# First two units behind each change of operands interleaved product by product, with weights and sums prepared in DRAM

## The chip, the cores and the metric

One core of one Trainium2 chip. The metric is the device time of the whole program in microseconds. The kernel before was run three times: 1918.71, 1915.92 and 1916.36 us, a median of 1916.36. One more execution was taken with the hardware profiler.

## The reference

A hybrid decoder layer on x (2048 tokens x 1024 channels, float32). One projection of the normalised input gives the parts of a gated short convolution, of a windowed attention, and of the merge gates; each branch is multiplied by a gate and projected back, and the merged result is projected once more.

```python
h = rms_norm(x, norm_g)
v_c, b_c, c_c, z_c, q, k, v, z_a, gate_logits = split(h @ w_in)
y_c = b_c * causal_depthwise_conv(c_c * v_c, conv_w) * silu(z_c)
y_a = y_c @ w_conv_out
o   = sliding_window_attention(rms(q), rms(k), v, sinks) * silu(z_a)   # window 128, 16 heads, 4 kv heads
y_b = o @ w_attn_out
g_a, g_b = split(sigmoid(gate_logits + gate_b))
return x + (g_a * y_a + g_b * y_b) @ w_out
```

## The kernel before

**Tiles and units.** The 2048 tokens are two tiles of T = 1024 (t = 0, 1). The work is a chain of units. A unit is 256 output channels for the 1024 tokens of a tile (in the last projection, o, 256 tokens for 1024 channels). Every float32 operand is split into a high part, rounded to fp32r by a cast on ScalarE (L279), and a low part, the rest, by a subtraction on VectorE; a product of two operands is hi.hi + hi.lo + lo.hi.

**Seven products or eight.** `sunit` (L493) is one level of Strassen's scheme in Winograd's form: seven products of half-size blocks, in the order 1, 5, 6, 2, 7, 3, 4. One product (`product`, L476, matmul L482) is 4 x 3 = 12 matmuls of 128x512. X, V and Y are banks of partial sums: product 1 goes to X and is copied by ScalarE to Y (L500); product 5 goes to V and is copied to s5 (L509); product 6 adds to Y, and VectorE sets V = s5 + Y; products 2, 7, 3 and 4 then complete the four blocks of the output, (0,0) in X, (1,1) as Y + s5, (0,1) in V and (1,0) in Y. The moving operands of the products are op 1, 2, 3 (plain blocks of the input) and op 5, 6, 7, 4 (their sums and differences), each of four pieces j = 0 to 3; "operand 2_3" is piece 3 of op 2. A plain unit is the ordinary block product: four outputs of two products, eight products and 96 matmuls, with op 1, 2, 3 and 8 (the fourth plain block).

**Changes of operands.** All units that share an input use one set of operands. At a change of input the set has to be formed anew: 28 or 32 splits and 16 sums. Per tile, and in this order (but for ga_0 of t = 0, which comes ahead of q), these are the units: k, v, q (on the normalised x), cv and b (with attention woven in), ga, gb, z, za (on the normalised x), then yb (the attention's output, operands ophc), then ya (the convolution's, operands ophy in t = 1; in t = 0 ya is the plain `branch`, L1255); after both tiles o (operands ophwo, from w_out; the merged rows are its weights). The first unit behind a change is plain, since that needs only plain blocks at first: yb_0 in both tiles (`yb_first`, L1279, matmul L1296), ya_0 in t = 1 and o_0 (`qunit`, L528, matmul L542). In t = 0 ga_0 is plain too.

**Order of the work.** The program is written out tick by tick: `run` (L676) gives one product of a unit per tick and calls what `put(n, f)` placed at that tick: operand splits, sums, loads. Tables of ticks (CSUM_AT, CONV_AT, WO_FORM_AT and others) place them. Beside that each tick prepares one piece of a coming unit's weights (`pieces_of`): from a raw tile of 1 MB, loaded by SP a unit or two ahead (L347), ScalarE casts 128x1024 high parts and VectorE subtracts the low parts (`ah`, `al` for products 1 and 2, `sh`, `sl` for 6 and 5, `th`, `tl` for 7 and 3, `d` for 4) and forms the sums. They live in eight tiles that are used in turn. Each engine then works its own list in order; a DMA issued by SP waits in SP's list for its data, and what stands behind it waits too.

**Ends of units.** yb's and ya's outputs are multiplied by a gate (th, loaded from gd in DRAM) and go to mt in DRAM: yb's by a store on SP (L1329), ya's by an accumulating DMA on POOL (L1331). The gate's tiles come from a pool of two. The last projection adds xr (a piece of x) and stores out (L1381). In t = 0's and t = 1's z and za units the attention of the tile's last blocks is still running (scores L1023, exponentials L1052, transposed through DRAM as fd, L1072 and L1079).

**The opening.** The statistics of x's norm are worked out in the first 40 us; TensorE transposes rtok (L609) so that rb can scale the tokens of a column block.

## Time and profile before

| what | value |
|---|---|
| runs | 1918.71, 1915.92, 1916.36 us (median 1916.36) |
| the profiled execution's own time | 1914.36 us |
| its span from the first to the last instruction | 1912.6 us |
| TensorE (PE) | 8718 matmuls |
| DMA | 371.79 MB, mean 194 GB/s |

Times in the views are microseconds from the span's start. In a row of the chain or the timeline the first number is the start, the second the duration; "x12" counts instructions, and what stands in brackets is the engine's idle time before the row and what ended it. In a row of the windows each engine's busy time is followed by its count of instructions, then the granted clock, the busy share of the DMA engines, and GB/s. L482 is line 482 of the kernel.

### The profile page before, as it was taken

How to read it: one execution, taken by the hardware profiler on the slowest of the kernel's cores; microseconds unless marked ns; L12 is line 12 of the kernel's file. 1: busy time of each engine (PE TensorE's matmuls, PEld its weight loads, DVE VectorE, ACT ScalarE, POOL GpSimd, SP SyncE). 2: the span in 40 equal slices, each digit the busy share in tenths (PEclk: the TensorE clock that was granted, in tenths of full speed). 3: DMA queues.
4: the chain of work that ended last, by engine and by line, in shares of the span. 5: the costliest groups of instructions: out<-in, count | busy, mean ns of one | idle time of the engine just before them, and what ended most of it. 6: DMA issues, size and time to landing. Idle time of an engine off the chain costs nothing.

```text
span 1912.6 us, 27255 instructions
## 1 busy us (share of the span) xinstructions
PE 1900.8 (99%) x8718; PEld 1581.7 (83%) x8718; DVE 1540.4 (81%) x2614; ACT 991.0 (52%) x1969; POOL 589.4 (31%) x850
## 2 busy tenths in 40 slices
PE   9999999999999999999999999999999999999999
PEld 7888888888887888888888888888888888888887
DVE  7988888898878669669799888888998578777854
ACT  7665555456657444434565544556666335434321
POOL 2083425345565000011462333445555001121000
PEclk9999999999999999999999999999999999999999
DMA  8286455558787433894585554567776674688453
GB/s 301 72 244 182 153 164 171 169 175 248 231 251 225 163 111 135 282 280 117 171 229 151 176 158 141 162 219 241 234 243 213 219 243 159 229 268 205 151 175 112
DMA packets 209279, 371.79 MB, mean 194 GB/s; under 512 B 28592, under 2 KB 103344, under 8 KB 199152
## 3 DMA queue, kind: packets, MB, share of 16 engines
q1 hardware_dynamic: 174688, 281.63, 44.9%
q0 software_dynamic: 30848, 79.99, 15.7%
q10 hardware_dynamic: 3600, 8.42, 1.3%
q8 instruction: 70, 1.15, 0.3%
q14 instruction: 73, 0.60, 0.1%
HBM read 252.22 MB, written 117.72 MB: 193 GB/s over the span
## 4 chain that ended last, share of the span: by engine, by line
PE 90%; DVE 4%; DMA 4%; issue 1%; ACT 0%; SPq 0%; POOL 0%; DVEq 0%; ACTq 0%; POOLq 0%
PE Y L482 33%; PE Vcv L482 4%; PE Xcv L482 4%; PE ya L1255 4%; PE Xgb L482 2%; PE Vq L482 2%; PE Xq L482 2%; PE yb L1296 2%; PE po L1117 2%; PE Vgb L482 2%; PE Vz L482 2%; PE Xz L482 2%; PE Vo L482 2%; PE Xo L482 2%; PE Vb L482 2%; PE Xb L482 2%
## 5 line engine op out<-in xcount | busy, mean ns | idle before, releaser
L1079 POOL DMA_DIRECT2D x<-fd x256 | 139.6, 552 | 120.5 <-DMA fd<-f 63.2
L1052 ACT ACTIVATE p<-s,st,rq 128x128 f32<-128x128 f32 x256 | 113.0, 450 | 5.4 <-DMA fd<-f 5.3
L1072 POOL DMA_DIRECT2D fd<-f x64 | 36.9, 576 | 229.1 <-DVE f L248 214.7
L1100 POOL TENSOR_SCALAR_AFFINE_SELECT xh<-xh 64x512 fp32r<-64x512 f32 x64 | 58.8, 919 | 147.4 <-DVE xl L248 104.4
L1351 POOL DMA_DIRECT2D mt<-tha x16 | 13.8, 860 | 257.6 <-DVE tha L248 244.3
L482 PE MATMUL Xcv<-oph,wcv_ah 128*128 128x512 f32 x256 | 79.2, 390 | 0.0
L1100 POOL TENSOR_SCALAR_AFFINE_SELECT xl<-xl 64x512 fp32r<-64x512 f32 x64 | 65.1, 1018 | 4.4
L1100 POOL TENSOR_SCALAR_AFFINE_SELECT yp<-yp 64x512 fp32r<-64x512 f32 x64 | 58.1, 908 | 4.2
L248 DVE TENSOR_TENSOR o<-po,o 64x256 f32<-64x256 f32 x128 | 53.3, 417 | 4.3 <-ACT o L1129 3.4
L1100 POOL TENSOR_SCALAR_AFFINE_SELECT yp<-xl 64x512 fp32r<-64x512 f32 x64 | 55.8, 872 | 3.1
L482 PEld LDWEIGHTS Xcv<-oph,wcv_ah 128*128 128x128 f32 x256 | 47.6, 188 | 9.6
L375 ACT CAST wcv_sh<-wcv_raw 128x1024 fp32r<-128x1024 f32 x16 | 16.8, 1052 | 70.5 <-DVE wcv_raw L248 70.5
L1817 POOL DMA_DIRECT2D oc<-ocd x16 | 8.7, 541 | 142.2 <-DMA th<-gd 118.9
L248 DVE SCALAR_TENSOR_TENSOR y<-u,cols,y 128x512 f32<-128x512 f32 x64 | 49.7, 776 | 3.4 <-ACT y L1166 2.2
L1129 ACT COPY o<-po 64x256 f32<-64x256 f32 x128 | 47.1, 368 | 8.3 <-PE po L1117 3.9
L248 DVE TENSOR_TENSOR p<-p,st 128x512 f32<-128x512 f32 x64 | 48.4, 756 | 3.1
L1052 ACT ACTIVATION_READ_ACCUMULATOR p<-s,st,rq 128x1 f32 x256 | 50.6, 198 | 0.0
L857 POOL DMA_DIRECT2D q2d<-q_h x64 | 44.2, 690 | 20.1 <-ACT q_h L852 11.0
L482 PE MATMUL Xcv<-oph,wcv_al 128*128 128x512 f32 x128 | 49.8, 389 | 0.0
L248 DVE TENSOR_TENSOR ophc<-zain,ophc 128x512 fp32r<-128x512 f32 x64 | 42.2, 687 | 7.1 <-ACT ophc L279 7.1
L248 DVE STREAM_TRANSPOSE f<-p 128x512 f32<-128x512 f32 x64 | 45.5, 711 | 3.0 <-DMA q<-q2d 0.2
L1027 PEld LDWEIGHTS s<-kq,q 128*128 128x128 f32 x256 | 45.9, 189 | 2.2
(698 smaller groups left out, 6539.3 us busy)
## 6 DMA issues: line engine op xcount, KB each, us to landing
gd<-th SPq DMA_DIRECT2D x64, 256.0 KB, 3.0
wcv_raw<-in_w_units SPq DMA_DIRECT2D x16, 1024.0 KB, 5.3
q<-q2d SPq DMA_DIRECT2D x64, 256.0 KB, 4.8
v<-vd SPq DMA_DIRECT2D x128, 128.0 KB, 3.4
fd<-f POOLq DMA_DIRECT2D x64, 256.0 KB, 4.3
x<-fd POOLq DMA_DIRECT2D x256, 64.0 KB, 3.3
th<-gd SPq DMA_DIRECT2D x48, 256.0 KB, 5.5
wga_raw<-in_w_units SPq DMA_DIRECT2D x8, 1024.0 KB, 7.0
```

What stands on the lines that cost most here:

```text
L248: r = f(*args, **kw)
L482: nc.tensor.matmul(ps, lhsT=w[:, j, :], rhs=b[:, m, :], start=start and j == 0 and i == 0, stop=j == KP - 1 and i == 2, skip_group_check=n ...
L857: nc.gpsimd.dma_start(q2d[t][j][half, q * 2 * HB : (q + 1) * 2 * HB, i, e, :], src[HALVES[e]].bitcast(F32).rearrange("p (b x) -> p b x", x ...
L1027: nc.tensor.matmul(sp[:, h, c, skip : 3 * HD], lhsT=q2[:, h, c, :], rhs=kq[:, 0, keys], start=False, stop=c == 1)
L1052: nc.scalar.activation(out=p[:, i, :], in_=sg[:, i, HD : 3 * HD], func=AF.Exp, bias=st[:, 1, i : i + 1], scale=rv[:, i // 2, i % 2 : i % 2 ...
L1072: nc.gpsimd.dma_start(fd, f)
L1079: nc.gpsimd.dma_start(x[QUADS[k]], src[k])
L1100: nc.gpsimd.affine_select(out=d4, in_=s4, pattern=[[0, 2], [-32 * sg, 2], [0, G], [-sg, 32]], compare_op=ALU.is_gt if prev else ALU.is_ge, ...
L1117: nc.tensor.matmul(po[:, cs], lhsT=v2[:, kind, :], rhs=xx[:, :, h * HD : (h + 1) * HD], start=n == 0, stop=n == 2)
L1129: nc.scalar.copy(ov, pov[oth, :, e])
L1255: nc.tensor.matmul(ps, lhsT=w[:, j, cs], rhs=o[:, m, :], start=n == 0 and i == 0, stop=n == KC - 1 and i == 2)
L1296: nc.tensor.matmul(banks[i, q], lhsT=w[:, j, :], rhs=b[:, l, :], start=n == 0 and m == 0, stop=n == KC - 1 and m == 2, skip_group_check=True)
```

## The change

**Pairs.** At each of the four changes (yb in t = 0 and 1, ya in t = 1, o) the first two units are run together by `spair`: product 1 of the first, product 1 of the second, then 2, 2, 5, 5, 6, 6, 3, 3, 7, 7, 4, 4. Both have seven products; op 8 isn't formed any more. The first unit uses the banks as before; the second has X and V in banks of the pool ps_m and its own bank for Y. ga_0 of t = 0 stays plain.

**Prepared weights.** In t = 0's z and za units `prepare` forms all high and low parts of yb_0's and yb_1's weights once (22 VectorE operations, 14 casts) and stores them in DRAM (wpd, 28 stores of 256 KB). The yb pairs of both tiles load them from there (kind "L", 14 loads of 512 KB a pair) in place of 1 MB raw a unit with casts and subtractions.

**Sums of w_out.** `wo_sums` forms them in t = 1's z and za units and stores them in DRAM (wsd); at the o change 28 pieces of 256 KB are loaded, each three ticks ahead of its split.

**Places.** The pieces of the weights of a pair alternate between its units. The second transposes of rtok move from tick 11 to 12, and the other places of the opening stay where they were, now in a table. Attention blocks 29 to 31 of t = 0 load a tick earlier. CSUM_AT, CONV_AT, WO_FORM_AT and the ticks of yb's operands (CA_...) have new numbers. `sunit` has a flag `last` for an order 1, 5, 6, 7, 2, 4, 3; it is given as `n + 1 == len(zs)`, after loops in the same body that set n to other values.

DMAs on SP: 1166 before, 1260 after; on POOL 580 and 576. VectorE has 2620 instructions after, 2614 before.

```diff
-TURNED_AT = (6, 11)
+TURNED_AT = (6, 12)
+WO_AHEAD = 3
+EARLY_LOADS = ((0, 29), (0, 30), (0, 31))
+PAIR = (1, 2, 5, 6, 3, 7, 4)
...
+    def prepare(key, n0, places):
...
+        def high(m, kh, over):
+            r = raw[kh]
+            hi = slot([P, H], F32R, f"wph_{w}_{j}_{m}")
+            lo = (r if over else slot([P, H], F32, f"wpl_{w}_{j}_{m}")).bitcast(F32R)
+            nc.scalar.copy(hi, r)
+
+            def low():
+                vec.tensor_tensor(out=lo, in0=r, in1=hi.bitcast(F32), op=ALU.subtract)
+                put(tick[0] + 1, keep)
+
+            def keep():
+                for l, v in enumerate((hi, lo)):
...
+                    nc.sync.dma_start(to, v.bitcast(F32))
+
+            put(tick[0] + 1, low)
...
+        if kind == "L":
+            made = wpd[key[0], key[2]]
+
+            def fetch(ms, i):
+                def go():
...
+                        tiles = wpair(f"{name}_{'ast'[i]}")
...
+                    for l, v in enumerate(tiles):
+                        nc.sync.dma_start(v.bitcast(F32), made[i][:, l])
+
+                put(tick[0] + 1, go)
+                return (lambda: None, lambda: None)
...
+    def spair(keys, ops, fins, order):
...
+        xb, vb, yb, s5 = [None, None], [None, None], [Y, None], [None, None]
+        for n, e in ((n, e) for n in order for e in range(2)):
+            u, fin, nm = us[e], fins[e], nms[e]
+            if n == 1:
+                xb[e] = (mb if e else bank)(f"X{nm}")
+                product(xb[e], u, 1, ops, True)
+                if e:
+                    yb[e] = bank(f"Y{nm}")
+                nc.scalar.copy(yb[e], xb[e])
+            elif n == 2:
+                product(xb[e], u, 2, ops, False)
+                fin(0, 0, xb[e])
+            elif n == 5:
+                vb[e] = mb(f"V{nm}")
+                product(vb[e], u, 5, ops, True)
+                s5[e] = spare(f"s5{nm}")
+                nc.scalar.copy(s5[e], vb[e])
+            elif n == 6:
+                product(yb[e], u, 6, ops, False)
+                add(vb[e], s5[e], yb[e])
...
+            yield
...
-    def yb_first(t, ops, fin):
...
+    def wo_sums(n, j):
...
+        def out(m, a, b, c):
+            sub(a, b, c)
+            nc.sync.dma_start(wsd[m, j], a)
...
+        for i, (m, j) in enumerate((m, j) for m in PAIR for j in range(KP)):
+            n = n1 + WO_FORM_AT[i]
+            put(n - WO_AHEAD, lambda m=m, j=j: ld(m, j))
+            put(n, lambda m=m, j=j: op_split("wo", m, j, got[m, j], st["ops"]))
...
-            put(n - 5, step("l", lambda g, j=j, b=b: att_load(t, j, b)))
+            put(n - 5 - ((t, r) in EARLY_LOADS), step("l", lambda g, j=j, b=b: att_load(t, j, b)))
...
-            run(sunit((key, t, j), ops, fin))
+            run(sunit((key, t, j), ops, fin, last=n + 1 == len(zs)))
...
-        run((sunit if n else qunit)(("o", n), state[NT]["ops"], fin))
+    run(spair([("o", e) for e in range(2)], state[NT]["ops"], [fins[e][0] for e in range(2)], PAIR))
...
+        run(sunit(("o", n), state[NT]["ops"], fin))
```

TensorE at the start of yb in t = 1, before the change: the end of the first and all of the second of the plain unit's last four outputs, yb_1_0, by op 1 and 2 (ophc) with the plain weights p1h and p1l, and the next unit's first product.

```order
L1296 MATMUL yb_1_0_15772<-ophc_1_0_15522,wyb_0_p1h 128x512 x2
L1296 MATMUL yb_1_0_15772<-ophc_1_0_15522,wyb_0_p1l 128x512
...
L1296 MATMUL yb_1_0_15772<-ophc_1_3_15615,wyb_0_p1h 128x512 x2
L1296 MATMUL yb_1_0_15772<-ophc_1_3_15615,wyb_0_p1l 128x512
L1296 MATMUL yb_1_0_15772<-ophc_2_3_15684,wyb_0_p1h 128x512 x2
L1296 MATMUL yb_1_0_15772<-ophc_2_3_15684,wyb_0_p1l 128x512
L482 MATMUL Xyb_1_15813<-ophc_1_0_15522,wyb_1_ah 128x512 x2
L482 MATMUL Xyb_1_15813<-ophc_1_0_15522,wyb_1_al 128x512
```

The same place after: products 1 and 1 are over with the first four rows, and product 2 of the first unit follows, up to operand 2_3.

```order
L632 MATMUL Xyb_1_15795<-ophc_1_2_15678,wyb_1_ah 128x512 x2
L632 MATMUL Xyb_1_15795<-ophc_1_2_15678,wyb_1_al 128x512
L632 MATMUL Xyb_1_15795<-ophc_1_3_15735,wyb_1_ah 128x512 x2
L632 MATMUL Xyb_1_15795<-ophc_1_3_15735,wyb_1_al 128x512
L632 MATMUL Xyb_0_15764<-ophc_2_0_15727,wyb_0_ah 128x512 x2
L632 MATMUL Xyb_0_15764<-ophc_2_0_15727,wyb_0_al 128x512
L632 MATMUL Xyb_0_15764<-ophc_2_1_15778,wyb_0_ah 128x512 x2
L632 MATMUL Xyb_0_15764<-ophc_2_1_15778,wyb_0_al 128x512
L632 MATMUL Xyb_0_15764<-ophc_2_2_15781,wyb_0_ah 128x512 x2
L632 MATMUL Xyb_0_15764<-ophc_2_2_15781,wyb_0_al 128x512
L632 MATMUL Xyb_0_15764<-ophc_2_3_15810,wyb_0_ah 128x512 x2
L632 MATMUL Xyb_0_15764<-ophc_2_3_15810,wyb_0_al 128x512
```

Operand 2_3 was read first at the end of the plain unit's sixth product and is now read at the end of the pair's third.

ScalarE around the cast of that operand, before (zas_7_0 is the gate that completes the last block of the attention's output):

```order
L1223 ACTIVATE zas_7_0_15630<-Y 128x512
L279 CAST ophc_2_2_15632<-zain_2_1_0_15286 128x512
L375 CAST wyb_1_ah<-wyb_1_raw 128x1024
L279 CAST ophc_8_3_15657<-zain_3_0_1_15418 128x512
L279 CAST ophc_3_3_15660<-zain_3_1_1_15416 128x512
L375 CAST wyb_1_d<-wyb_1_raw 128x512
L279 CAST ophc_2_3_15684<-zain_3_1_0_15420 128x512
```

And after:

```order
L1427 ACTIVATE zas_7_0_15750<-Y 128x512
L303 CAST ophc_5_2_15752<-zain_2_0_0_15397 128x512
L704 COPY Y<-Xyb_0_15764 128x512
L303 CAST ophc_2_1_15778<-zain_1_1_0_15256 128x512
L303 CAST ophc_2_2_15781<-zain_2_1_0_15403 128x512
L303 CAST ophc_3_3_15789<-zain_3_1_1_15545 128x512
L704 COPY Yyb_1_15808<-Xyb_1_15795 128x512
L303 CAST ophc_2_3_15810<-zain_3_1_0_15549 128x512
```

The casts of weights are gone from the place, and the two copies of X into Y now stand between the casts of operands.

SP in the yb pair of t = 1, after (wpd holds the prepared weights, gd the gates, mt takes the products of yb's outputs and gates):

```order
L484 DMA wyb_1_sh<-wpd_yb_1_5959 128x1024
L484 DMA wyb_1_sl<-wpd_yb_1_5959 128x1024
L1495 DMA th_0_1_15792<-gd_1_119 128x512 x2
L1508 DMA mt_115<-th_0_0_15761 128x512 x2
L484 DMA wyb_0_th<-wpd_yb_2_5956 128x1024
L484 DMA wyb_0_tl<-wpd_yb_2_5956 128x1024
L1495 DMA th_0_2_15881<-gd_1_119 128x512 x2
L484 DMA wyb_1_th<-wpd_yb_2_5960 128x1024
L484 DMA wyb_1_tl<-wpd_yb_2_5960 128x1024
L484 DMA wyb_0_d<-wpd_yb_3_5957 128x1024
L1508 DMA mt_115<-th_0_1_15792 128x512
```

The same place before:

```order
L347 DMA wyb_2_raw<-in_w_units 128x2048
L1317 DMA th_0_0_15637<-gd_1_118 128x512 x2
L1317 DMA th_0_1_15664<-gd_1_118 128x512 x2
L1329 DMA mt_114<-th_0_0_15637 128x512 x2
L1329 DMA mt_114<-th_0_1_15664 128x512
L1317 DMA th_1_0_15785<-gd_1_118 128x512 x2
L1329 DMA mt_114<-th_0_1_15664 128x512
L347 DMA wyb_3_raw<-in_w_units 128x2048
```

One raw load of 1 MB per unit, two units ahead, gave way to loads for the pair itself, some of which stand behind stores of the same pair.

More of the change, by code (lines that the diff above doesn't have):

```diff
@@ L513, in sunit @@
         yield
-        if not two:
+        if not two and not last:
             product(xb, u, 2, ops, False)
@@ L520, in sunit @@
         yield
[L521 to L523 removed]
+        if last:
+            product(xb, u, 2, ops, False)
+            fin(0, 0, xb)
+            yield
+        else:
+            product(vb, u, 3, ops, False)
+            fin(0, 1, vb)
+            yield
         product(Y, u, 4, ops, False)
@@ L1333, in y_unit @@
-        if j:
-            return sunit(key, ops, fin), get
-        return (yb_first(t, ops, fin) if w else qunit(key, ops, fin)), get
+            last = shared and n == len(order) - 1
+            pair = None if last else upool.tile([P, 2 * H + 2], F32, tag="u", name=f"th{w}{t}_{js[0]}_{n}")
+            for e, (j, i, q) in enumerate(order[n]):
+                th[j, i, q] = slot([P, H], F32, f"th{w}{t}_{j}_{n}") if last else pair[:, hs(e)]
+                nc.sync.dma_start(th[j, i, q], gd[t][w][2 * j + i, :, hs(q)])
@@ new lines, in y_ends, with y_units @@
+        return [fin_of(j) for j in js], get
+    def y_units(t, w, ops):
+        key = "yb" if w else "ya"
+        order = PAIR
+        outs = pair_outs(order)
+        fins, get = y_ends(t, w, (0, 1), outs)
+        units = [(spair([(key, t, j) for j in range(2)], ops, fins, order),
+                  get, ((0, 0), (1, 1), (outs[0][0] + 1, 2), (THS_AT, 3)), outs[1][0] + 1)]
+        for j in range(2, NJ):
+            (fin,), get = y_ends(t, w, (j,), None)
+            units.append((sunit((key, t, j), ops, fin), get, ((0, 0), (1, 1)), 7))
+        return units
@@ L1767, in block_kernel @@
         zs[0][3]()
+        if t + 1 == NT:
+            for j in range(KP):
+                wo_sums(tick[0] + WO_SUMS_AT[j], j)
+        if t == 0:
+            for j in range(2):
+                prepare(("yb", j), tick[0], (PREP_A, PREP_B)[j])
         def csum(n, j):
```

479 lines of the change are left out of this document (294 added, 185 removed).

## The prediction

> **What bounds the kernel now.** I read the page's busy shares first, then the chain that ended last, then TensorE's waits, then windows around the four places that the change touches.
>
> ```profile
> span 1912.6 us, 27255 instructions
> ...
> PE 1900.8 (99%) x8718; PEld 1581.7 (83%) x8718; DVE 1540.4 (81%) x2614; ACT 991.0 (52%) x1969; POOL 589.4 (31%) x850
> ...
> PE 90%; DVE 4%; DMA 4%; issue 1%; ACT 0%; SPq 0%; POOL 0%; DVEq 0%; ACTq 0%; POOLq 0%
> ```
>
> PE is busy for 1900.8 of 1912.6 us, so 11.8 us is all its idle time, and the chain runs through it. A matmul that goes is time that goes, as long as the operands keep up. The chain at the changes of operands (the one of t=1 in full) shows whether they do:
>
> ```profile
> 725.07 21.76 PE yb L1296 x96
> ...
> 1596.12 21.76 PE yb L1296 x96
> 1617.88 2.72 PE Xyb L482 x12
> 1620.60 2.72 PE Vyb L482 x12
> ...
> 1675.00 21.76 PE Qya L542 x96
> ...
> 1753.88 21.76 PE Qo L542 x96
> ```
>
> Each plain unit takes 21.76 us for 96 matmuls, 0.2267 us each, and a product of 12 takes 2.72 us. Rows follow without a gap: 1596.12 + 21.76 = 1617.88. The windows say the same, and show how near VectorE is to its limit there:
>
> ```profile
> core 0: us, PE busy (x) PEld busy (x) DVE busy (x) ACT busy (x) POOL busy (x), PEclk, DMA share, GB/s
> ...
> 725.00:763.00 38.00, 38.00 (x170) 31.45 (x169) 36.30 (x57) 17.65 (x30) 0.00 (x0) 1.00 0.38 132
> ...
> 1596.00:1634.00 38.00, 38.00 (x169) 31.49 (x168) 36.31 (x57) 17.71 (x30) 9.73 (x18) 1.00 0.64 224
> ...
> 1675.00:1713.00 38.00, 38.00 (x169) 31.45 (x169) 27.44 (x41) 12.76 (x21) 10.97 (x17) 1.00 0.85 260
> 1713.00:1754.00 41.00, 41.00 (x183) 33.94 (x182) 29.20 (x42) 20.42 (x31) 8.54 (x10) 1.00 0.96 246
> 1754.00:1792.00 38.00, 38.00 (x169) 31.48 (x168) 36.41 (x57) 13.09 (x21) 0.85 (x1) 1.00 0.49 143
> ```
>
> PE has no idle time and a full clock in any of them; VectorE is busy for 36.3 of 38 us. So the question is what feeds the shorter stretch.
>
> **Term 1, the matmuls.** Four plain units of eight products become units of seven: 4 x 12 = 48 matmuls, 8718 to 8670, at 0.2267 us: **-10.88 us**. Two units now take 14 products, 14 x 2.72 = 38.08 us, where they took 40.80.
>
> **Term 2, the opening.**
>
> ```profile
> 38.99 0.62 PE L609 MATMUL ptr<-ident,rtok 128*128 128x128 f32 x4 [1.52 <-DVE rtok L603]
> ...
> 67.85 0.69 DVE L248 TENSOR_TENSOR oph<-xt,oph 128x512 fp32r<-128x512 f32 x1
> ...
> 68.73 0.61 PE L542 MATMUL Qga<-oph,wga_p0h 128*128 128x512 f32 x2
> ```
>
> The second transposes of rtok stand 12 matmuls later (2.7 us), past the 1.52 us that PE waited for rtok. But VectorE's low part of operand 3_3 ends at 68.54, and the matmul that reads it is the second of the pair at 68.73, about 68.96. VectorE's chain is not shortened, so with PE 1.5 us earlier this operand is about 1 us late. Between 0 and -1.5; I take **-0.5 us**.
>
> **Term 3, the pairs' own operands.** Their times come from walking each engine's new order from the pair's start, with these durations:
>
> ```profile
> 1674.40 1.66 ACT L279 CAST ophy<-oc 128x512 fp32r<-128x512 f32 x3
> ...
> 1675.64 1.89 DVE L248 TENSOR_TENSOR ophy<-oc,ophy 128x512 fp32r<-128x512 f32 x3
> ...
> 1677.44 1.22 DVE L248 TENSOR_TENSOR wya_al<-wya_raw,wya_ah 128x1024 fp32r<-128x1024 f32 x1
> ...
> 1678.58 0.69 DVE L248 TENSOR_TENSOR ophy<-oc,ophy 128x512 fp32r<-128x512 f32 x1
> ...
> 1699.51 0.57 ACT L500 COPY Y<-Xya 128x512 f32<-128x512 f32 x1 [4.29 <-PE Xya L482]
> ```
>
> Back to back, a VectorE operation of 128x512 takes (1.89 - 0.69) / 2 = 0.60 us, one of 128x1024 1.14 (1677.44 to 1678.58), a cast 0.52; a copy starts 0.03 us behind its product's end (1699.48) and takes 0.57.
>
> In the yb pair VectorE has 51 operations, three of them 128x1024: 48 x 0.60 + 3 x 1.14 = 32.2 of 38.08 us. It had 36.3 in 38. Weight work left (prepared in t=0), so on the mean it keeps up. The tight point is the place shown for ScalarE: the copy of X into the new bank Yyb stands ahead of operand 2_3's cast. Product 1 of the second unit ends at 5.44; copy to 6.04, cast to 6.6, low part to 7.4; its reader, the 11th matmul of product 2, stands at 5.44 + 10 x 0.2267 = 7.71. That leaves 0.3 us, where the plain unit read 2_3 only in its sixth product. Operand 4_1 comes out at 33.6 against 33.5. Both yb pairs: 0 to 1 us; I take **+0.4**.
>
> Their loads: VectorE's and ScalarE's work on two units' weights becomes 14 loads of 512 KB. The later ones wait on SP behind stores of mt that wait for VectorE; in before such stores held SP 31 times, for 112.3 us in all and 15.9 at most:
>
> ```profile
> SPq L1329 <- DVE th L248: 112.3, 31, 15.9
> ```
> ```profile
> wya_raw<-in_w_conv_out SPq DMA_DIRECT2D x8, 512.0 KB, 7.1
> ...
> wya_raw<-in_w_units SPq DMA_DIRECT2D x4, 1024.0 KB, 7.2
> ...
> wo<-in_w_out SPq DMA_DIRECT2D x16, 256.0 KB, 6.9
> ```
> ```profile
> xr<-in_x SPq DMA_DIRECT2D x32, 256.0 KB, 4.0
> ...
> oc<-csd POOLq DMA_DIRECT2D x16, 256.0 KB, 5.1
> ```
>
> By the walk wyb_0_th goes out at about 11.7 (behind the store that needs product 2 of the second unit, 10.88) and is needed at 21.76; wyb_1_th at 14.6, needed at 24.48; wyb_1_d at 25.5, needed at 35.36. Each has about 10 us, and 512 KB landed in 7.1: no cost, with 3 us to spare.
>
> The ya pair (t=1) still forms its weights. Its narrow point is the last low part of operand 7_3, at 28.9 against 29.5, behind the cast of the third unit's weights, whose load goes out at 15.2. At 7.2 us it fits, at 10 us VectorE's queue would end 2.5 late: 0 to 2.5, I take **+0.5** (nearer the 7.2).
>
> The o pair: operand 7_3's load goes out at about 16.4, behind a store that waits for product 2 of the second unit and VectorE's queue. With 5.1 us it lands at 21.5; cast, low part, 4_2's low part, a 128x1024 one and the sum for V follow (0.6 + 0.7 + 0.6 + 1.1 + 0.7) to 25.2, where product 3 of the second unit wants V at 24.48: 0.7 late. With 4.0 us nothing is late, with 6.9 it is 2.5. Operand 4_0, loaded behind the next weights, adds 0 to 1.5. So 0 to 4; DMA is at 0.49 in that window of before, so I take 5.1 and 0.5: **+1.2**.
>
> [...]
>
> **Term 4, what is made ahead.** The weights of yb_0 and yb_1 get 22 VectorE operations (13 us) and 14 casts in t=0's z and za units, with 2 MB loaded and 7.3 MB stored; w_out's 16 sums (10 us) and 8 MB move to t=1's.
>
> ```profile
> 620.00:660.00 40.00, 40.00 (x181) 33.23 (x180) 23.22 (x33) 15.49 (x25) 3.31 (x4) 1.00 0.59 210
> 660.00:700.00 40.00, 40.00 (x179) 33.10 (x178) 22.01 (x29) 14.56 (x22) 0.00 (x0) 1.00 0.29 106
> ...
> 1460.00:1500.00 40.00, 40.00 (x186) 33.43 (x185) 29.27 (x40) 19.60 (x33) 10.05 (x13) 1.00 0.54 179
> 1500.00:1540.00 40.00, 40.00 (x178) 32.86 (x177) 25.40 (x36) 14.13 (x22) 0.00 (x0) 1.00 0.72 249
> ```
>
> From 620 to 700 VectorE is free for 34.8 us and the DMA engines for more than half; from 1460 to 1540 it is free for 25. The cover is there. SP gets 34 and 24 more DMAs at 0.33 us each:
>
> ```profile
> 1699.29 0.33 SPq L347 DMA_DIRECT2D wya_raw<-in_w_units  x1
> ```
>
> That is 19 us over some 250; behind them stand only loads for the next unit, 19 us ahead of it (seven products). Were the cover gone, the last attention blocks would pay, as one did before:
>
> ```profile
> 575.28 0.46 ACT L1052 ACTIVATE p<-s,st,rq 128x128 f32<-128x128 f32 x1 [5.30 <-DMA fd<-f]
> ...
> 577.21 0.44 PE L1023 MATMUL s<-lows,kq 128*128 128x384 f32 x1 [2.18 <-ACT p L1052]
> ```
>
> This 2.18 us can go (three blocks of t=0 load a tick earlier) or come twice: -2.2 to +2.2, I take **0**.
>
> **Sum.** -10.88 - 0.5 + 0.4 + 0.5 + 1.2 + 0 = **-9.3 us**. The profiled execution took 1914.36 (span 1912.6 and 1.8 outside it): 1905.1. The runs shown have a median of 1916.36, 2.0 above it; on that basis **1907.1 us**. The terms at their best give -10.88 - 1.5 - 2.2 = -14.6 (1901.8), at their worst -10.88 + 1 + 2.5 + 4 + 2.2 = -1.2 (1915.2).
>
> **Rivals.** *The operands of the pairs are late, and most of the gain is stall.* A set of four operands is now due every 5.44 us, and each pair has a place with under 0.7 us to spare; if VectorE runs 1.5 us behind my walk at each pair (its queue is in order, so a delay stays), the four pairs lose 6 and the o pair its 2 to 4 more: -10.88 + 9 = about -2, **1914.5**. For it: VectorE's 36.3 of 38 us before. Against it: the 6 us less that it now has. Chance 0.11.
>
> *The prepared weights' loads land too late, and it is slower.* Place: the 512 KB loads issued from 11.7 on in the two yb pairs.
>
> ```profile
> 1626.00:1636.00 10.00, 10.00 (x46) 8.28 (x45) 9.83 (x15) 3.16 (x6) 4.25 (x9) 1.00 1.00 364
> ```
>
> The DMA engines were already full once in that stretch, at 364 GB/s. Each load has 10 us; product 3 and then, issued later for it, product 4 wait for what is over that, so a pair loses 2 x (L - 10) for a landing of L. It is slower than before from L = 10 + 9.3 / 4 = 12.3 us, and by over 0.2% from 13.3; at 16 us it is 24 - 9.3: **1931**. Against it: 7.1 us for 512 KB, and 4 MB of oc loads that stood in that window now start later. Chance 0.07.
>
> *The change does less than it says*: the opening gives back its 1.5 us and the order with a last product moved in za's last unit does not take effect (its flag compares a loop variable that inner loops have set anew, and the new order shows the old products). Both are in the sum already; **1907.6**, inside the forecast.
>
> *The clock falls in the pairs.* They rotate over six banks of partial sums. In this trace the clock was 1.00 in every window, and a wait of 2.18 us did not lower it. If a stall halved it for one product behind it, each would cost 1.36 us, in four pairs with two stalls 11: **1918**, within 0.2%. [...] Chance 0.02.
>
> **How the numbers follow.** Forecast 0.80, rivals 0.11, 0.07 and 0.02. A measurement here tells about 0.2% (3.8 us) from no change: faster means below 1912.5, slower above 1920.2. The forecast is faster but for its worst corner (0.03), the late operands divide (0.03 faster, 0.08 same), the clock is same, the loads slower, and 0.01 of the same is moved to slower for what I have not seen: faster 0.80, same 0.12, slower 0.08. The range takes in the terms' ends, 1902 to 1915.
>
> **What would show it.** PE x8670 and about 1890 us busy; chain rows of 2.72 through all four pairs, 38.08 us each; TensorE's idle time near 13 us, with its waits in the pairs on ophc's low part, on Vo and on ophwo 7_3 or 4_0. Waits of PE on wyb loads would make the slower rival; waits over 2 us on VectorE in each pair the first; a wait near 69 us on oph shows the opening giving back.

## The result and the profile after

| | before | after |
|---|---|---|
| median of the runs | 1916.36 us (9 runs, 1913.82 to 1918.71) | 1911.87 us (9 runs, 1909.72 to 1915.00) |
| ratio | | 0.9979, 95% interval 0.9970 to 0.9988 |
| profiled execution, its span | 1914.36, 1912.6 us | 1912.3, 1910.6 us |

The change gains 4.5 us, 0.2%. The sign and the main term are as forecast, the size is half: -9.3 was expected. First the page of the kernel after, its busy times and the engines' shares of the chain:

```profile
span 1910.6 us, 27374 instructions
...
PE 1894.5 (99%) x8670; PEld 1574.3 (82%) x8670; DVE 1541.5 (81%) x2620; ACT 986.5 (52%) x1967; POOL 588.1 (31%) x846
...
PE 86%; DVE 6%; issue 3%; DMA 3%; ACT 1%; POOL 0%; SPq 0%; DVEq 0%; POOLq 0%; ACTq 0%
```

The 48 matmuls are gone (8718 to 8670), which is 10.9 us of work, but PE's busy time fell by only 6.3 us (1900.8 to 1894.5) and its idle time rose from 11.8 to 16.1. So some matmuls became slower, and some waits are new. The waits of TensorE name them (total, times, longest):

```profile
PE s L1227 <- ACT p L1256: 3.4, 1, 3.4
PE Y L632 <- DVE zs L272: 1.8, 1, 1.8
PE Y L1681 <- DVE zero L191: 1.5, 1, 1.5
PE Y L632 <- DVE ophy L272: 1.3, 1, 1.3
PE Yyb L632 <- DVE wyb_raw L272: 1.0, 1, 1.0
...
PE Qga L746 <- DVE oph L272: 0.5, 2, 0.3
...
PE Y L632 <- DVE ophc L272: 0.4, 2, 0.2
```

The waits on zs, ophy and Yyb are new, and so are the short ones on oph and ophc. The windows of the four pairs (yb in t = 0 and t = 1, ya, o) show which of them run without a gap:

```profile
core 0: us, PE busy (x) PEld busy (x) DVE busy (x) ACT busy (x) POOL busy (x), PEclk, DMA share, GB/s
722.00:760.00 38.00, 38.00 (x170) 31.39 (x168) 34.28 (x55) 18.27 (x32) 0.00 (x0) 1.00 0.69 228
1598.00:1636.00 38.00, 36.74 (x161) 29.79 (x160) 33.54 (x53) 16.63 (x29) 9.20 (x17) 1.00 0.88 321
1676.00:1714.00 38.00, 36.69 (x162) 30.08 (x161) 31.26 (x46) 16.70 (x27) 9.05 (x13) 1.00 0.72 204
1753.00:1792.00 39.00, 39.00 (x173) 31.99 (x172) 33.66 (x51) 17.44 (x27) 1.71 (x2) 1.00 0.84 256
...
1477.00:1484.00 7.00, 5.30 (x16) 4.21 (x17) 6.93 (x9) 0.56 (x1) 4.38 (x4) 0.76 0.81 266
```

The windows at yb of t = 0 and at o are full (the first ends 5 us before its pair does, and one wait of 0.22 us, at 760.58, lies behind it); yb of t = 1 and ya miss 1.3 us each. The last row is no pair: in z of t = 1 TensorE stands for 1.7 us and the granted clock falls to 0.76. Cut into stretches, each from the first matmul of a stage to the first of the next, the two profiled executions differ like this (us):

| stretch | before | after | difference |
|---|---|---|---|
| opening, up to cv of t = 0 | 156.62 | 155.88 | -0.74 |
| z, za of t = 0 | 162.52 | 164.97 | +2.45 |
| yb of t = 0 | 78.88 | 76.78 | -2.10 |
| z, za of t = 1 | 157.52 | 160.59 | **+3.07** |
| yb of t = 1 | 78.88 | 78.04 | -0.84 |
| ya of t = 1 | 78.88 | 77.76 | -1.12 |
| o, to its last matmul | 155.04 | 152.59 | -2.45 |
| the other four | 1040.41 | 1039.96 | -0.45 |

A pair alone would take 2.72 us (12 matmuls) off its stage. The rows sum to -2.2, less than the medians' -4.5, because the execution of before that was profiled lay 2.0 us under its median, and that of after 0.4 over its own. The +2.45 in t = 0 is one wait near 577 us (3.38 us in after) and the slow product behind it (4.32), and its length need not be the change's: the code up to there is the same in before and in the clock probe below, and they show 2.18 and 2.90 us there, and 2.77 and 4.17 us for the product behind the wait (z and za 162.52 and 164.04); over all profiled executions this wait ranges from none to 4.23.

**The wait in z of t = 1.** SP's list, VectorE's and TensorE's, one fence each:

```profile
1468.36 0.88 SPq L1581 DMA_DIRECT2D wos<-in_w_out  x2
```
```profile
1476.63 0.69 DVE L272 TENSOR_TENSOR wos<-wos 128x512 f32<-128x512 f32 x1 [5.24 <-DMA wos<-in_w_out]
...
1477.96 0.69 DVE L272 TENSOR_TENSOR zs<-Y,s5z 128x512 f32<-128x512 f32 x1
```
```profile
1478.70 4.62 PE L632 MATMUL Y<-oph,wz_d 128*128 128x512 f32 x12 [1.78 <-DVE zs L272]
```

The first sum of w_out waits 5.24 us for its load, issued 8 us before. VectorE works its list in order, so zs, which frees Y, stands behind it, and product 4 waits for zs. Then the product itself takes 4.62 us in place of 2.72, at the lower clock of the window above. Wait and product together cost 1.78 + 1.90 = 3.7 us; without them the stage would take 156.9.

**The wait in yb of t = 1.** SP sends the last load of the pair's weights, and product 4 of the second unit reads it:

```profile
1625.56 0.42 SPq L484 DMA_DIRECT2D wyb_d<-wpd_yb  x1
```
```profile
1635.31 2.99 PE L632 MATMUL Yyb<-ophc,wyb_d 128*128 128x512 f32 x12 [1.03 <-DVE wyb_raw L272]
```

The profile puts this wait down to a VectorE operation long done; in six of the experiments the same wait is named "DMA wyb_d". The load was issued at 1625.56 and landed 9.6 us later.

**The wait in ya.** ScalarE's list around the third unit's weights, and the low part of operand 7_3 that comes out late:

```profile
1700.51 1.05 ACT L463 CAST wya_ah<-wya_raw 128x1024 fp32r<-128x1024 f32 x1 [4.13 <-DMA wya_raw<-in_w_units]
1701.47 2.69 ACT L303 CAST ophy<-oc 128x512 fp32r<-128x512 f32 x5
```
```profile
1705.79 0.50 PE L632 MATMUL Y<-ophy,wya_th 128*128 128x512 f32 x1 [1.31 <-DVE ophy L272]
```

Here too an engine stands in its list at a load (4.13 us), and the casts of operands wait behind it.

### The profile page after: what moved, and what is told of

It reads as the page before. It is cut to its first block, busy times and chain, and to the rows that moved or that the text cites. A ratio compares the mean times of both kernels' runs of the same rounds, so it can differ in the third digit from the quotient of the medians.

```text
span 1910.6 us, 27374 instructions
## 1 busy us (share of the span) xinstructions
PE 1894.5 (99%) x8670; PEld 1574.3 (82%) x8670; DVE 1541.5 (81%) x2620; ACT 986.5 (52%) x1967; POOL 588.1 (31%) x846
## 4 chain that ended last, share of the span: by engine, by line
PE 86%; DVE 6%; issue 3%; DMA 3%; ACT 1%; POOL 0%; SPq 0%; DVEq 0%; POOLq 0%; ACTq 0%
PE Y L632 32%; PE Vcv L632 4%; PE Xcv L632 4%; PE ya L1459 4%; PE Xgb L632 2%; PE Vq L632 2%; PE Xq L632 2%; PE Vo L632 2%; PE Xo L632 2%; PE Xza L632 2%; PE Vza L632 2%; PE po L1321 2%; PE Vgb L632 2%; PE Vz L632 2%; PE Xz L632 2%
## 5 line engine op out<-in xcount | busy, mean ns | idle before, releaser
L272 DVE TENSOR_TENSOR ophc<-zain,ophc 128x512 fp32r<-128x512 f32 x56 | 37.4, 688 | 17.2 <-ACT ophc L303 17.1
L1061 POOL DMA_DIRECT2D q2d<-q_l x64 | 44.1, 689 | 15.1 <-DMA q2d<-q_h 8.7
```

The source lines that it names most:

```text
L272: r = f(*args, **kw)
L1061: nc.gpsimd.dma_start(q2d[t][j][half, q * 2 * HB : (q + 1) * 2 * HB, i, e, :], src[HALVES[e]].bitcast(F32).rearrange("p (b x) -> p b x", x ...
```

## The experiments

**Theory A**: the miss is three waits at loads. In each, an engine's in-order list (VectorE's in z, ScalarE's in ya, TensorE's own in yb) holds work that waits for a transfer, ahead of work that TensorE needs. **Rival B**: VectorE has too little time left there, and a wait that is taken away comes back a little later. **Rival C**, for the sums: they cost time at any place. In the recorded expectations the letters are each run's own. Before was run again beside these kernels, with medians of 1915.4 to 1916.2, and the ratios are to those.

### The sums of w_out later behind their loads

```diff
-WO_SUMS_AT = (2, 8, 16, 27)
+WO_SUMS_AT = (2, 11, 20, 29)
...
-        put(n + 3, lambda: out(0, two[0][0], two[0][1], two[0][0]))
+        put(n + 6, lambda: out(0, two[0][0], two[0][1], two[0][0]))
...
```

> Theory A (VectorE's own list is blocked): in the changed kernel the first of w_out's sums for j = 1 stood in VectorE's list while its load was still under way (idle 5.24 us before the row at 1476.63), the subtraction zs behind it came late, TensorE waited 1.78 us and ran at half clock for most of the next product (4.62 in place of 2.72). With the sums three ticks (some 8 us) behind where they were and the loads of the later pieces 3 to 4 ticks later, that wait and the slow product go: 3.7 us less, about 1908.2 against the changed kernel's 1911.9, and t = 1's z and za units have no product of over 3 us. Rival B (the 8 MB of extra transfers make attention's round trips late, wherever the sums stand): the wait moves to another place in the z units and the time stays within 1 us of 1911.9.

Measured: 1913.43 us (11 runs), ratio 0.9992 (0.9983 to 1.0000). The wait at zs is gone, and z and za of t = 1 take 160.84, not less. TensorE and VectorE in za:

```profile
1536.28 3.02 PE L632 MATMUL Y<-oph,wza_d 128*128 128x512 f32 x12 [2.00 <-DVE zas L272]
...
1551.56 0.73 PE L632 MATMUL Y<-oph,wza_th 128*128 128x512 f32 x2 [1.39 <-DVE Vza L272]
```
```profile
1535.53 0.69 DVE L272 TENSOR_TENSOR zas<-Y,s5za 128x512 f32<-128x512 f32 x1 [4.82 <-DMA ocd<-zin]
```

The cost moved by one unit, as rival B says. Theory A's number is refuted, and here its form is too: VectorE waits for no load of w_out in this kernel. Before zas it stood for the landing of a store (ocd); SP had sent such stores just ahead of and just behind a load of w_out. So the transfers, the rival of the expectation, are not ruled out by this run. Beside that, the wait on ophy in ya is 1.94 us here, and ya takes 80.27 us (77.76 after).

### The third ya unit's piece held, and the last yb load at once

Two kernels. In the first, the piece whose cast stood at the load starts three ticks later; in the second, product 4's load is sent in its own tick, ahead of the store of mt.

```diff
+HOLD = 3
...
+    held = [0]
...
+        if (plan[n][2], i) == (("ya", 1, 2), 0) and held[0] < HOLD:
+            held[0] += 1
+            return None
```
```diff
-                put(tick[0] + 1, go)
+                if len(ms) == 1:
+                    go()
+                else:
+                    put(tick[0] + 1, go)
```

> Theory A: in the ya pair the cast of the third unit's weights (wya_2_ah) stood on ScalarE ahead of operand 7's four casts and waited 4.13 us for its load; with that piece held for three ticks the casts of operand 7 come first, the wait of 1.31 us of TensorE at product 7 goes and the ya stretch (from its start to o's) shrinks by 1.5 us, from 77.8 to about 76.3: 1910.4. Rival B (operand 7's own pieces come late from POOL's loads): the wait at product 7 stays at 1 us or more.

Measured: 1910.33 us (6 runs), ratio 0.9969 (0.9957 to 0.9981). The wait of 1.31 is gone, ya takes 77.34 (77.76 after). So the cast was the cause of that wait, but the stage gained 0.4 us where 1.5 was expected; that the time came out as expected (1910.4) is luck. In the profiled execution the larger gain is in z and za of t = 0, 160.39 (164.97 after), without a wait near 577. A shorter wait is new:

```profile
1747.81 3.06 PE L638 MATMUL Y<-ophy,wya_d 128*128 128x512 f32 x12 [0.84 <-DVE s5ya L273]
```

> Theory A: the last weights of the second unit of a yb pair (wyb_1_d) were loaded behind the store of the first output and two loads of gates, went out at 27.4 us of the pair, landed 9.6 us later and held TensorE for 1.03 us in t = 1. Given out one tick earlier, ahead of that store, the load has 5 to 6 us more and the wait at the last product goes in t = 1, 1.2 us less there; in t = 0, where no wait stood at that place, nothing changes: 1910.7. Rival B (the wait is VectorE's, as the row names wyb_raw): it stays.

Measured: 1909.79 us (5 runs), ratio 0.9967 (0.9954 to 0.9979). The wait is gone and yb of t = 1 takes 76.75 (78.04 after), as yb of t = 0 does. Theory A holds for the load: sent ahead of that store and of the gates' loads behind it, it is in time.

### What a wait costs in clock

In before, V = s5 + Y of product 6 is repeated 5, 6, 7, 8, 10 and 12 times in o_2 to o_7, so that product 7 waits for a set time. The sum is the same each time, so the output does not change.

```diff
-        add(vb, s5, Y)
+        for _ in range({2: 5, 3: 6, 4: 7, 5: 8, 6: 10, 7: 12}.get(key[1], 1) if key[0] == "o" else 1):
+            add(vb, s5, Y)
```

> The kernel before, in which the sum V = s5 + Y of the o units 2 to 7 is formed 5, 6, 7, 8, 10 and 12 times in a row in place of once (the same value each time, so the output is unchanged). Product 7 has to wait for the last, so TensorE should wait about 0.60 us for each repeat less some 2.5 us of slack: 0.5, 1.1, 1.7, 2.3, 3.5 and 4.7 us. Theory A (a wait over some length costs the clock): short waits leave the next product at 2.72 us, longer ones make it 4 to 4.6 us, with one length between them from which on it happens. Rival B (the wait's length doesn't decide; the waits of 1.52 and 2.18 us of the kernel before had no slow product behind them, one of 1.78 us after the change had): slow products come without order in the lengths. Rival C (the slow products have another cause than the wait): none here is slow, whatever the wait.

Measured: 1944.81 us in one execution. Three of the products with their waits, and then the same three in the chain, where the second number is the product's whole length:

```profile
1829.23 0.73 PE L482 MATMUL Y<-ophwo,wo_th 128*128 128x512 f32 x2 [1.78 <-DVE Vo L248]
...
1851.07 0.95 PE L482 MATMUL Y<-ophwo,wo_th 128*128 128x512 f32 x2 [2.51 <-DVE Vo L248]
...
1875.26 1.22 PE L482 MATMUL Y<-ophwo,wo_th 128*128 128x512 f32 x2 [3.24 <-DVE Vo L248]
```
```profile
1829.23 3.02 PE Y L482 x12
...
1851.07 4.60 PE Y L482 x12
...
1875.26 4.62 PE Y L482 x12
```

Behind waits of 1.05 and 1.78 us the product takes 3.01 and 3.02; behind 2.51 and 3.24, 4.60 and 4.62; behind 4.70 and 6.16, 5.38 and 5.12. So a wait of 2.5 us costs about 4.4. Within this execution that is theory A's form, a bound between 1.78 and 2.51 us. But in after, 1.78 us at 1478.70 was enough for 4.62, so there is no one bound. Rows of the other profiled executions, behind the opening: after waits of 1.03 to 1.39 us matmuls ran at full rate again after the first (12 of them took 2.99 us behind the 1.03 of after), one case apart, of 1.31 us just behind another of 2.27, with 0.43 us a matmul in place of 0.227 (the sums in k, v, q). Behind waits of 1.78 to 3.38 us the rate was halved for a while in most cases (the clock was 0.50 from 1480 to 1482 in after, and a matmul took 0.43 us), and not behind 2.00 us (the sums later, 12 matmuls in 3.02), 2.18 (before, at 577, 2.77), 2.41 (the load at once and the piece held, without the additions), 2.43 (the sums on GpSimd) and 3.32 (the sums in k, v, q). Behind 3.84 us (yb's weights formed again), 4.23 (all three edits) and 4.78 (the sums in k, v, q) it was halved too, with 0.43 us a matmul or 4.61 for 12. Why waits of one length have either effect is not shown.

### The sums in another stage, and without VectorE

```diff
-WO_SUMS_AT = (2, 8, 16, 27)
+WO_SUMS_AT = (5, 11, 17, 23)
...
-        if t + 1 == NT:
-            for j in range(KP):
-                wo_sums(tick[0] + WO_SUMS_AT[j], j)
...
         tick0 = tick[0]
+        if t == 0:
+            for j in range(KP):
+                wo_sums(tick[0] + WO_SUMS_AT[j], j)
```

The sums stand at ticks 5, 11, 17 and 23 of t = 1's k, v and q.

> w_out's sums (16 VectorE operations, 8 loads and 16 stores) stand in t = 1's k, v and q units in place of its z and za units. Theory A (they cost the 3 us that t = 1's z and za units are longer after the change, 160.6 against 157.5, in every changed kernel so far 160.3 to 162.1): the z and za stretch goes back to 157.5 and k, v and q stay at 116.3, as VectorE and the DMA engines have room there: 1908.8. Rival B (the stretch is longer for another reason, the new places of csum's pieces or of yb's operands): it stays at 160 or more, and so does the time. Rival C (the cost moves along): k, v and q grow by 2 to 3 us.

Measured: 1928.32 us (5 runs), ratio 1.0058 (1.0045 to 1.0070). z and za of t = 1 take 157.25, 3.3 less than after: A is right on what the sums cost there. But k, v and q grow from 116.40 to 133.33: the cost moves along, as C says, and is 17 us where C said 2 to 3. One of the four waits:

```profile
951.95 4.61 PE L632 MATMUL Y<-oph,wq_d 128*128 128x512 f32 x12 [4.78 <-DVE q_t L272]
```

Ahead of q_t VectorE had stood for 6.09 us at k_t, whose load (krb) was under way; at a sum it stood once in this stage, for 4.3 us. SP's list, in which the next pieces of w_out wait for the stores of the last ones, stood for 21.1 us at that (8.6 at most). Why the whole is 17 us is open.

In the next kernel the transfers stay and the 16 additions are left out (the stored pieces are then plain blocks of w_out, so the output is not the reference's):

```diff
         def out(m, a, b, c):
-            sub(a, b, c)
             nc.sync.dma_start(wsd[m, j], a)
```

> The sums of w_out are left out (the raw pieces are stored in their place), while their loads, stores and places in t = 1's z and za units stay. Theory A1 (an operation that waits for its load blocks VectorE's list): the wait of VectorE on wos goes and z and za take 157 to 158 us. Rival A2 (the transfers themselves, on SP's list and on the DMA engines, make the loads and stores of the z units late): 160 us or more still, with waits of VectorE or ScalarE on other DMAs there.

Measured: 1909.50 us (4 runs), ratio 0.9965 (0.9952 to 0.9979); z and za of t = 1 at 156.88, with the same 8 MB moved. So the transfers alone do not cost the 3.7 us; it takes the additions. But three things go with the additions: the block at the load, some 10 us of VectorE's time, and the waits of SP for the sums that it is to store. From 1437 to 1600 us of after these waits are:

```profile
SPq L1586 <- DVE wos L272: 19.0, 14, 4.0
```

Which of the three costs what, this run does not show. For the wait on zs the rows of after show the block.

All three edits together (sums in k, v, q; the load at once; the piece held):

> The three edits together: w_out's sums in t = 1's k, v and q units, the last weights of the yb pair's second unit loaded a tick earlier, and the ya pair's cast of the third unit's weights held for three ticks. If the stretches add up as measured one by one (z and za of t = 1 3.1 less, yb of t = 1 1.3 less, ya 1.0 less): 1911.9 - 5.4 = 1906.5. If the freed waits come back behind it (later operands on the same engines): 1909 or more.

Measured: 1927.66 us (5 runs), ratio 1.0057 (1.0045 to 1.0070). z and za 156.87, yb 76.77 and ya 77.09 are regained, and k, v, q (134.92) loses more than that.

### What carries the pairs

yb's first two units form their weights again, as the other units do; everything else stays.

```diff
-            if j < 2:
-                plan[-1] = ("L",) + plan[-1][1:]
...
-        if t == 0:
-            for j in range(2):
-                prepare(("yb", j), tick[0], (PREP_A, PREP_B)[j])
```

> No prepared weights: the yb pairs form both units' weights from raw tiles as the ya pair does, and the work and the transfers of the preparation in t = 0's z and za units go. Theory A (the prepared weights are what lets VectorE keep up): VectorE has 32.2 + some 10 us of work in a pair's 38, so TensorE waits 2 to 5 us in each yb pair, and each yb stretch takes 79 to 82 us in place of 76.8 and 78.0: 1916 to 1919. Rival B (the weights' pieces find room ahead of the pair, as in the ya pair): the stretches stay below 78.5 and the time is 1911 to 1912. t = 0's z and za units should not be shorter by more than 0.5 us, since the preparation stood beside idle time.

Measured: 1933.28 us (4 runs), ratio 1.0088 (1.0072 to 1.0103). The yb stages take 87.98 and 89.22: 11 us more each, well over what either theory of the expectation said (79 to 82, or below 78.5), with waits such as

```profile
741.98 0.79 PE L632 MATMUL Xyb<-ophc,wyb_ah 128*128 128x512 f32 x1 [3.84 <-DVE ophc L272]
```

The prepared weights are what makes the pair pay in yb. z and za of t = 0, free of their preparation, take 164.32, in the middle of what the kernels with it take (160.4 to 167.0): that preparation is covered, as far as the wait near 577 lets one see.

### The sums on GpSimd, later on VectorE, and no early loads

```diff
-WO_SUMS_AT = (2, 8, 16, 27)
+WO_SUMS_AT = (15, 23, 31, 39)
...
-            sub(a, b, c)
+            sub(a, b, c, nc.gpsimd)
```

> w_out's 16 sums are formed on GpSimd instead of VectorE, and start at ticks 15, 23, 31 and 39 of t = 1's z and za units, when attention's last blocks are over and GpSimd has nothing to do. Theory A1 (what costs 3 us there is VectorE's list, blocked by operations that wait for their loads): z and za of t = 1 take 157 to 158 us as in the kernel before and without the sums, and the time is 1911.9 - 3.2 = 1908.7. Rival A3 (an operation of GpSimd on the same pieces slows VectorE's own, or the stores held for it delay SP's loads): 159 us or more.

Measured: 1913.59 us (11 runs), ratio 0.9989 (0.9980 to 0.9998); z and za of t = 1 at 162.66, 2 us more than after, as A3 says. GpSimd's sums, what VectorE does beside them, and TensorE:

```profile
1537.46 1.29 POOL L310 TENSOR_TENSOR wos<-wos 128x512 f32<-128x512 f32 x1 [18.36 <-DMA cr<-ocd]
1538.83 3.33 POOL L310 TENSOR_TENSOR wos<-wos,wos 128x512 f32<-128x512 f32 x2
```
```profile
1536.79 5.91 DVE L272 TENSOR_TENSOR wza_raw<-wza_raw 128x512 f32<-128x512 f32 x4
1542.62 2.29 DVE L272 TENSOR_TENSOR wza_sl<-wza_raw,wza_sh 128x1024 fp32r<-128x1024 f32 x1
```
```profile
1544.96 0.50 PE L632 MATMUL Vza<-oph,wza_sl 128*128 128x512 f32 x1 [2.43 <-DVE wza_sl L272]
```

In after the same two groups, with GpSimd idle, take half:

```profile
1537.03 2.75 DVE L272 TENSOR_TENSOR wza_raw<-wza_raw 128x512 f32<-128x512 f32 x4
1540.11 1.23 DVE L272 TENSOR_TENSOR wza_sl<-wza_raw,wza_sh 128x1024 fp32r<-128x1024 f32 x1 [0.34 <-ACT wza_sh L463]
```

So here work put on GpSimd was not out of VectorE's way: beside the sums VectorE needed 5.91 and 2.29 us in place of 2.75 and 1.23.

With the other two edits added:

> The sums on GpSimd as in the run before, the last weights of the yb pair's second unit loaded a tick earlier, and the ya pair's cast of the third unit's weights held for three ticks. By the stretches: z and za of t = 1 157.3, yb of t = 1 76.8, ya 77.2: 1911.9 - 3.2 - 1.3 - 0.8 = 1906.6. If what is freed comes back behind it: 1908.5 or more.

Measured: 1910.47 us (10 runs), ratio 0.9969 (0.9960 to 0.9978). yb and ya are regained (76.79, 77.01), z and za are not (162.12).

The same late ticks on VectorE:

> The control for the run with GpSimd: the sums stay on VectorE, with the same later ticks 15, 23, 31 and 39. Theory A1: VectorE's list is still blocked by the loads and z and za of t = 1 take 159.5 us or more. Rival (the place beside attention's last blocks was the trouble, not the engine): 157 to 158 us, as on GpSimd.

Measured: 1912.90 us (10 runs), ratio 0.9983 (0.9974 to 0.9992); z and za 160.60, with a new wait of 1.82 us of TensorE on Vza. VectorE ahead of it:

```profile
1539.99 1.41 DVE L272 TENSOR_TENSOR wos<-wos,wos 128x512 f32<-128x512 f32 x2
...
1544.87 0.68 DVE L272 TENSOR_TENSOR wos<-wos 128x512 f32<-128x512 f32 x1
...
1548.48 0.69 DVE L272 TENSOR_TENSOR Vza<-s5za,Y 128x512 f32<-128x512 f32 x1
```

The number is A1's (159.5 or more), the cause is not: no sum waits for its load here. From 1539.38 on VectorE works without a gap, three sums among it, and so comes late to Vza. At these ticks it is rival B's case, too little time.

And without the three early loads of the attention in t = 0 (`EARLY_LOADS = ()`):

> Attention blocks 29 to 31 of t = 0 load at their old ticks again. If the earlier loads are what made the round trip of fd longer (8.61 us against 7.41) and the wait at 577 us longer (3.38 against 2.18): t = 0's z and za units take 162.5 us in place of 164 to 165, and the time falls by 1.5 us. If those differ from one execution to the next whatever the loads do (the probe, a kernel before, had a wait of 2.90 there and 164.0): no change beyond 0.7 us.

Measured: 1912.43 us (11 runs), ratio 0.9979 (0.9970 to 0.9988), as after; the wait at 577 is 2.04 us in its profile, 3.38 in after's. The early loads decide nothing that can be measured.

### Whether the three losses add up

First the load at once and the piece held, with the sums as in the change:

> The loads of product 4's weights sent at once and the third ya unit's piece held 3 ticks, both; the sums of w_out as in the change. Theory A (three separate losses: sums about 3 us, the yb load 1.3, the ya piece 0.8 to 1.3; each regained alone, so both together give both): 1911.9 - 2.1 - 1.5 = 1908.3, yb of t=1 at 76.8 and ya at 77.3 us, z and za of t=1 still at 160 to 162. Rival B (the later stage takes back what the earlier one gains, since VectorE's list there is as long as before): no better than either alone, about 1910.

Measured: 1910.43 us (6 runs), ratio 0.9971 (0.9959 to 0.9982); yb of t = 1 at 76.77, ya at 76.92, z and za at 159.45. The stretches of yb and ya are as theory A says. The time is not below that of either edit alone (rival B's number), but its interval holds theirs; whether the two add up is not decided by the time.

The same without the 16 additions:

> As the one before, and the 16 sums of w_out are left out on VectorE (the transfers stay; the stored pieces are plain ones, so the output isn't the reference's). Theory A: 1908.3 - 2.4 = 1905.9, z and za of t=1 at 156.9, within 1.5 us of the 1907.1 forecast, so the three losses are all that the forecast missed. Rival B: 1908 or more, and another loss has to be looked for.

Measured: 1906.94 us (5 runs), ratio 0.9951 (0.9937 to 0.9964): 8.9 us under before, where -9.3 had been forecast; the expectations' 1905.9 (A) and 1908 or more (B) lie on either side. The window of the old wait, with the sums left out:

```profile
1477.00:1484.00 7.00, 7.00 (x35) 5.88 (x35) 6.92 (x10) 4.42 (x7) 2.07 (x2) 1.00 0.87 313
```

TensorE is busy throughout, at a full clock. With the three losses gone the forecast's gain is there, within 0.4 us, but in a kernel that leaves out the additions; the change as it stands cannot have it.

The sums in t = 1's ga and gb units, each two ticks later behind its load, with the two other edits:

```diff
-WO_SUMS_AT = (2, 8, 16, 27)
+WO_SUMS_AT = (5, 17, 29, 41)
...
-        put(n + 3, lambda: out(0, two[0][0], two[0][1], two[0][0]))
+        put(n + 5, lambda: out(0, two[0][0], two[0][1], two[0][0]))
...
+        if t + 1 == NT:
+            for j in range(KP):
+                wo_sums(tick[0] + WO_SUMS_AT[j], j)
         for w, key in enumerate(("ga", "gb")):
...
```

> As the first, with the sums of w_out formed in t=1's ga and gb units (ticks 5, 17, 29, 41, two ticks later behind their loads), where VectorE is busy for 16.5 to 18.5 of 20 us and the DMA engines for 0.73 to 0.84. Theory A with cover there: z and za of t=1 at 156.9, cv to gb of t=1 within 0.5 us of 429.4, 1905.9. Rival C (no stage of this kernel has room for sums that wait for loads, since TensorE follows VectorE's list within a product everywhere): cv to gb grows by 2 us or more and the time stays at 1908 or above.

Measured: 1909.28 us (5 runs, 1907.23 to 1914.21), ratio 0.9968 (0.9956 to 0.9981). z and za of t = 1 take 156.88, fully regained, but in the profiled execution, its longest, cv to gb take 437.10 (429.41 after). There VectorE, then TensorE:

```profile
1372.42 0.69 DVE L273 TENSOR_TENSOR xl<-x,xh 128x512 fp32r<-128x512 f32 x1 [6.09 <-DMA od<-o]
```
```profile
1376.65 0.48 PE L1330 MATMUL po<-yp,v 128*128 128x256 f32 x1 [1.87 <-POOL yp L1313]
```

The attention's parts come late, and the clock drops behind the wait (0.83 from 1365 to 1385, with 0.43 us a matmul from 1378.82 on). By both its signs, this stage's growth and a median above 1908, the run is rival C's; of the other four executions, 1907.2 to 1909.5, one lies under 1908 and none at theory A's 1905.9. The fastest kernels that form the sums (this one, and the load sent at once, 1909.79) have intervals that overlap each other's; against after they gain 2 to 3 us.

## Why the prediction was off

**The matmuls** (-10.88): right. There are 8670, and yb of t = 0 gains 2.1 of its 2.72 us. The chain there runs gapless until it first leaves TensorE:

```profile
726.78 10.91 PE Xyb L632 x48
737.69 5.44 PE Vyb L632 x24
743.13 2.73 PE Y L632 x12
```

**The opening** (-0.5): right, -0.74. The stall on rtok is gone and two waits on oph came, as the step said, not at 68.96 but at 66.89 and 68.09, of 0.26 and 0.23 us.

**The yb pairs' operands** (+0.4): it was 1.2, so 0.8 more. In yb of t = 0, and of t = 1 with the load mended, the stage takes 76.77 where 78.88 - 2.72 = 76.16 would be free of loss: 0.6 each. The wait seen there is 0.22 us on ophc, at operand 4_1, where the walk was 0.1 short; with the slow start behind it that product of 12 takes 0.53 us more than 2.72. Operand 2_3 behind the copy of X was in time.

**The yb loads** ("no cost, with 3 us to spare"): wrong by 1.3 us, the difference that the load sent at once makes. The pair of t = 1 begins at 1598.2, so product 4's load went out at 27.4 where 25.5 was forecast, and took 9.6 us where 7.1 was taken; the window shows 0.88 of the DMA engines busy, with the gates' and the convolution's loads in it. The rival on these loads had the mechanism, at far too high a price: one load was late, not the whole set.

**The ya pair** (+0.5): the place and the cause were right (the cast of the third unit's weights ahead of operand 7_3's), the stage lost 1.6. The load went out at 15.6 (15.2 forecast) and landed after some 8.6 us, where the step had chosen 7.2 in a range up to 10.

**The o pair** (+1.2): too dear by 0.9. The stage lost 0.27 of its 2.72, within the range of 0 to 4. V of the second unit was ready in time, by this sum on VectorE:

```profile
1777.24 0.69 DVE L272 TENSOR_TENSOR Vo<-s5o,Yo 128x512 f32<-128x512 f32 x1
```

The pair begins at 1753.98, so V is ready at 23.95, where 25.2 was forecast and 24.48 needed. The 0.27 us lie in product 4 of the first unit, which takes 2.99 in place of 2.72:

```profile
1786.79 2.99 PE Y L632 x12
```

For a load of 256 KB the step took 5.1 us, out of 4.0 to 6.9; the median of these loads on SP was 6.0:

```profile
wo<-wsd SPq DMA_DIRECT2D x14, 256.0 KB, 6.0
```

**What is made ahead** (0): this is the step that failed. "The cover is there" counted VectorE's free time (25 us between 1460 and 1540 for 10 us of sums) and, for SP's list, what stands behind the new DMAs. It did not ask what stands behind the new sums in VectorE's own list while they wait for their loads. That cost 3.1 us in z and za of t = 1 against before, 3.7 against the kernel without the additions. Its sentence on SP's list was wrong too: behind the new DMAs stand not only loads for the next unit but stores and loads of the convolution and the attention (ocd, od, csd, cr). And moving the sums does not mend it: beside the attention's last blocks they cost as much without a wait for their own loads, once at a store that had not landed and once by VectorE's time alone. For t = 0 nothing speaks against the 0, as far as the wait near 577, which moves that stage by several us, lets one see.

**Falling clock.** The rival said that a stall might halve the clock of a product, and gave it 0.02, since 2.18 us had not done so. One did, of 1.78 us (a clock of 0.50 behind it, from 1480 to 1482), but in z and not in a pair; the two pairs' windows without a gap are at a clock of 1.00, so nothing points to the rotation of banks. It cost 1.90 us, where the rival had 1.36 for a stall; that is part of the 3.1.

**Sum**, from the profiles: 3.1 (sums) + 0.8 and 1.3 (yb) + 1.1 (ya) - 0.9 (o) - 0.25 (opening) = 5.1 us too little, against 4.8 in the medians. That they agree so well is partly luck: the wait at 577, left out here, moves single executions by more.

## What to carry to other kernels

Before work is put into the free time of an in-order engine, find out what it waits for and what stands behind it: free time in a window (25 of 80 us in before) was no cover for an operation that waits for a transfer (5.24 us at a sum of w_out), nor for work that stands right ahead of what TensorE needs (1.82 us at Vza with the late ticks). Count a load with its landing in the busiest window that it meets, not with the median of a quieter one (9.6 us here, where 7.1 was taken), and send it ahead of stores that wait (1.3 us here). A stall of some 2 us or more on TensorE is to be priced with the product behind it: 1.78 us came to 3.7 in after and 2.51 to 4.4 in the clock probe, though 1.78 and 2.00 elsewhere came to no more than 0.3 beside themselves.

## What the hardware showed

Two things were not expected. Behind waits of TensorE from 1.78 us on the next product mostly ran at half rate (12 matmuls in 4.62 us in place of 2.72 behind 1.78 in after, in 4.60 behind 2.51 in the clock probe), behind those of 3.84 to 6.16 us in all five cases, while waits of 1.03 and 1.05 us cost 0.3 us beside themselves (2.99 and 3.01). And beside sums on GpSimd VectorE's operations took twice as long (5.91 us for four in place of 2.75), and z and za of t = 1 took 162.66 us, where the same late ticks on VectorE gave 160.60.
